# Column sums of an 8192x8192 matrix: summing rows on VectorE in fp32 instead of bf16 matmuls for every block, with the last two blocks in column strips

## Chip, cores, metric

The kernel runs on one core of one Trainium2 chip. The metric is device time in microseconds (us), the median of the executions. The profile's span runs from the first to the last instruction and is about 1.85 us shorter than the time (644.0 against 645.85 in the profiled run of before). The experiments ran on three chips, each beside the kernel before, so where two kernels differ by little, their ratios to before are the fairer measure.

Engines: PE is TensorE's matmuls, PEld its weight loads, DVE is VectorE, ACT is ScalarE, SPq is the queue on SyncE that issues the loads and stores. "Landing" is the moment when a load's data can be used. The "granted clock" is TensorE's clock as a share of full speed. PSUM is the memory in which the matmuls' sums stand here, SBUF that of all other tiles.

## The reference

```python
def setup_inputs():
    return {"x": np.random.randn(8192, 8192).astype(np.float32)}

def reference(x):
    return np.sum(x, axis=0)
```

The input has 268.4 MB. It has to be read once, and nothing else of size moves.

## The kernel before

Rows are taken in 64 blocks of 128, one row per partition, so that a block is 128x8192 fp32, 4 MiB. ScalarE and VectorE cast it to bf16, and TensorE sums over the partitions with a column of ones, adding all blocks up in PSUM.

```python
load_pool = ctx.enter_context(tc.tile_pool(name="loads", bufs=4))
bf_pool = ctx.enter_context(tc.tile_pool(name="bf", bufs=3))
# ... cut: other pools; ones is [128, 1] bf16, psum is [128, 4096] fp32 ...
nsplit = 4
CS = C // nsplit
for i in range(n_row_blocks):                      # 64 blocks
    xt = load_pool.tile([P, C], mybir.dt.float32)
    xb = bf_pool.tile([P, C], mybir.dt.bfloat16)
    nc.sync.dma_start(out=xt, in_=xr[i])
    for s in range(nsplit):                        # casts, ScalarE and VectorE in turn
        # ... cut: eng.copy / eng.tensor_copy of xb[:, s*CS:(s+1)*CS] ...
    for g in range(n_col_groups):                  # 16 groups of 512 columns
        # ... cut: groups 0-7 go to partition 0, groups 8-15 to partition 64 ...
        nc.tensor.matmul(out=psum[opart : opart + 1, off : off + N], lhsT=ones,
                         rhs=xb[:, g * N : (g + 1) * N],
                         start=(i == 0), stop=(i == n_row_blocks - 1))

res = out_pool.tile([P, HALF], mybir.dt.float32)
nc.vector.tensor_copy(out=res[0:1, :], in_=psum[0:1, :])
nc.scalar.copy(out=res[64:65, :], in_=psum[64:65, :])
nc.sync.dma_start(out=out[0:HALF], in_=res[0:1, :])
nc.sync.dma_start(out=out[HALF:C], in_=res[64:65, :])
```

## Time and profile before

| what | value | where it is read |
|---|---|---|
| time | 645.85 us (645.6 to 646.63) | the runs |
| first block lands | 13.09 us | timeline, first cast |
| from one landing to the next | 9.72 us, mean 9.74 | timeline, starts of the casts |
| last block lands | 626.86 us | chain of waits |
| from there to the end | 17.1 us | span minus landing |

These are lines of the page of before. In the first group the columns are busy time, its share of the span, and the count. The row of digits gives the busy share of the 16 DMA engines in 40 equal slices, in tenths.

```profile
span 644.0 us, 2724 instructions
PE 336.7 (52%) x1024; PEld 97.4 (15%) x1024; DVE 155.6 (24%) x129; ACT 241.6 (38%) x130; POOL 0.3 (0%) x5
...
DMA  9999999999999999999999999999999999999970
...
q1 hardware_dynamic: 9220, 268.47, 97.0%
...
DMA 88%; ACT 5%; issue 4%; PE 1%; DVE 1%; SPq 0%; ACTq 0%
```

The loads are the bound: the DMA row is full until the last two slices, PE, the busiest compute engine, is busy for only 52%, and the chain of what released what is DMA for 88%. At 9.72 us per 4 MiB block the loads run at 431 GB/s.

The end of the chain of waits of before (start, duration, what):

```profile
591.73 35.03 DMA xt<-in_x_dram
...
626.86 1.91 ACT xb L50
...
628.81 4.50 PE psum L60 x15
...
633.34 4.42 DVE res L69
...
637.78 3.56 ACT res L70
```

After the last landing at 626.86 everything is in series: casts, matmuls, two copies that each run along a single partition, and the last store, 2.6 us from its issue at 641.37 to the end.

### The profile page before, as it was taken

The page shows a single profiled execution, that of the slowest core. Times are in us where ns is not written, and L with a number is a line of the kernel's source. Part 1 is how long each engine was busy: PE and PEld are TensorE (multiplying, and loading weights), DVE is VectorE, ACT ScalarE, POOL GpSimd, SP SyncE. Part 2 cuts the span into 40 slices and gives each one's busy share as a digit, 9 for nine tenths or more (in the row PEclk, how much of TensorE's full clock was granted, in tenths as well). Part 3 has the DMA queues.
Part 4 walks back from the last instruction along what each step waited for, and adds up shares of the span by engine and source line. Part 5 has one row for each costly group of instructions (what it writes and reads, how often), then busy time and mean ns, then how long its engine had stood idle before and what let it go on. Part 6 is the DMA issues. An engine that isn't in the chain of part 4 may idle for free.

```text
span 644.0 us, 2724 instructions
## 1 busy us (share of the span) xinstructions
PE 336.7 (52%) x1024; PEld 97.4 (15%) x1024; DVE 155.6 (24%) x129; ACT 241.6 (38%) x130; POOL 0.3 (0%) x5
## 2 busy tenths in 40 slices
PE   1464653655545644654646546635555547446533
PEld 0111111111111111111111111101111111111110
DVE  1122122222221221221221221221221221222223
ACT  2243243342442442442442432433433433433423
POOL 0000000000000000000000000000000000000000
PEclk9767668667767687678676766676678676876686
DMA  9999999999999999999999999999999999999970
GB/s 387 427 423 440 435 427 423 444 432 426 426 440 434 422 429 442 429 425 433 438 429 427 434 431 432 429 436 434 426 429 430 438 427 430 429 438 429 434 339 2
DMA packets 9233, 268.64 MB, mean 417 GB/s; under 512 B 1026, under 2 KB 1026, under 8 KB 1026
## 3 DMA queue, kind: packets, MB, share of 16 engines
q1 hardware_dynamic: 9220, 268.47, 97.0%
q8 instruction: 8, 0.13, 0.1%
q14 instruction: 5, 0.04, 0.0%
HBM read 268.44 MB, written 0.03 MB: 417 GB/s over the span
## 4 chain that ended last, share of the span: by engine, by line
DMA 88%; ACT 5%; issue 4%; PE 1%; DVE 1%; SPq 0%; ACTq 0%
DMA xt<-in_x_dram 88%; ACT xb L50 5%; PE psum L60 1%; DVE res L69 1%; ACT res L70 1%; SPq L46 0%; ACTq L50 0%
## 5 line engine op out<-in xcount | busy, mean ns | idle before, releaser
L60 PE MATMUL psum<-xb,ones 128*1 128x512 bf16 x1024 | 336.7, 570 | 296.6 <-DVE xb L52 290.7
L50 ACT CAST xb<-xt 128x2048 bf16<-128x2048 f32 x128 | 236.7, 1896 | 391.8 <-DMA xt<-in_x_dram 391.8
L52 DVE CAST xb<-xt 128x2048 bf16<-128x2048 f32 x128 | 151.2, 1224 | 478.0 <-DMA xt<-in_x_dram 478.0
L60 PEld LDWEIGHTS <-ones 128*1 128x1 bf16 x1024 | 97.4, 107 | 535.3 <-issue 521.9
L70 ACT COPY res<-psum 1x4096 f32<-1x4096 f32 x1 | 3.6, 3564 | 7.2 <-DVE res L69 7.2
L69 DVE COPY res<-psum 1x4096 f32<-1x4096 f32 x1 | 4.4, 4411 | 4.1 <-PE psum L60 4.1
L50 ACT ACT_TABLE_LOAD x1 | 1.3, 1283 | 0.7 <-PEq L87 0.7
L37 POOL MEMSET ones<- 128x1 bf16 x1 | 0.1, 102 | 0.3 <-POOLq L87 0.3
L87 POOL MEMSET const-bfloat16-1.0<- 128x1 bf16 x1 | 0.1, 102 | 0.0
L87 POOL MEMSET const-uint8-127<- 128x1 uint8 x1 | 0.1, 102 | 0.0
L87 POOL MEMSET const-float32-0.0<- 128x1 f32 x1 | 0.1, 99 | 0.2 <-issue 0.2
L87 POOL MEMSET const-float32-1.0<- 128x1 f32 x1 | 0.1, 99 | 0.0
## 6 DMA issues: line engine op xcount, KB each, us to landing
xt<-in_x_dram SPq DMA_DIRECT2D x64, 4096.0 KB, 35.0
out_dram<-res SPq DMA_DIRECT2D x2, 16.0 KB
```

The lines of the kernel that those rows point to most:

```text
L37: nc.gpsimd.memset(ones, 1.0)
L50: eng.copy(out=xb[:, s * CS:(s + 1) * CS], in_=xt[:, s * CS:(s + 1) * CS])
L52: eng.tensor_copy(out=xb[:, s * CS:(s + 1) * CS], in_=xt[:, s * CS:(s + 1) * CS])
L60: nc.tensor.matmul(out=psum[opart : opart + 1, off : off + N], lhsT=ones, rhs=xb[:, g * N : (g + 1) * N], start=(i == 0), stop=(i == n_row ...
L69: nc.vector.tensor_copy(out=res[0:1, :], in_=psum[0:1, :])
L70: nc.scalar.copy(out=res[64:65, :], in_=psum[64:65, :])
L87: nc = _bacc.Bacc("TRN2", target_bir_lowering=False, num_devices=1)
```

## The change

Its intent: take the casts and matmuls out of the stream, keep the sum in fp32, and shorten the end. VectorE adds each block to an accumulator of 128x8192 fp32, in four adds of 2048 columns. Fp32 matmuls with ones sum over the partitions only at the end. The last two blocks are loaded together, as column strips of 4, 2, 1, 0.5 and 0.5 MiB, so that little work is left after the last landing. Each matmul has 32 equal output rows and goes to one of four groups of 32 partitions ("column groups" of TensorE, the index `j`), so that 512 columns end as 128 elements on each of four groups.

```diff
-    load_pool = ctx.enter_context(tc.tile_pool(name="loads", bufs=4))
-    bf_pool = ctx.enter_context(tc.tile_pool(name="bf", bufs=3))
+    load_pool = ctx.enter_context(tc.tile_pool(name="loads", bufs=3))
...
+STRIPS = [(0, 8), (8, 4), (12, 2), (14, 1), (15, 1)]      # first unit, units of 512 columns
+    xl = x[n_acc * P :, :].rearrange("(p k) c -> p k c", k=2)   # last two blocks, n_acc = 62
+    ones = const_pool.tile([P, 32], F32)
+    psum = psum_pool.tile([P, n_banks * 512], F32)         # one tile, four banks
+    acc = const_pool.tile([P, C], F32)
+    last = last_pool.tile([P, 2, C], F32)
...
+    first = None
+    for t in range(n_acc):
+        xt = load_pool.tile([P, C], F32, tag="xt")
+        nc.sync.dma_start(out=xt, in_=xr[t])
+        if t == 0:
+            first = xt
+            continue
+        other = first if t == 1 else acc
+        for b in range(n_banks):
+            nc.vector.tensor_tensor(out=acc[:, cols], in0=other[:, cols], in1=xt[:, cols], op=add)
+    for u0, nu in STRIPS:
+        nc.sync.dma_start(out=last[:, :, cols], in_=xl[:, :, cols])
+    for b in range(n_banks):          # accumulator: 16 fp32 matmuls of 512 columns
+        for j in range(NJ):
+            mm(v[:, j], j, 512 * b, 512, True, False)
+    for u0, nu in STRIPS:
+        # strips of 4 units or more: one add of the two rows on VectorE, then matmuls;
+        # narrower ones: matmuls for both rows
+        ...
+        nc.vector.tensor_copy(out=res[:, 128 * u0 : 128 * (u0 + nu)],
+                              in_=psum[:, 128 * u0 : 128 * (u0 + nu)])
+        nc.sync.dma_start(out=outr[:, u0 : u0 + nu, :], in_=res[0 : 97 : 32, ...])
```

(The diff is cut and its long lines are shortened; the casts, the bf16 matmuls and the two long copies of before are gone.)

More of the change, by code (lines that the diff above doesn't have):

```diff
@@ L7 @@
 from concourse._compat import with_exitstack
+F32 = mybir.dt.float32
+BANK = 2048
+NQ, NJ, NI = 4, 4, 128
+STRIPS = [(0, 8), (8, 4), (12, 2), (14, 1), (15, 1)]
 @with_exitstack
@@ L19 @@
     R, C = x.shape
-    assert R % P == 0
-    n_row_blocks = R // P
-    N = 512
-    assert C % N == 0
-    n_col_groups = C // N
-    HALF = C // 2
+    assert R % P == 0 and C % BANK == 0
+    n_blocks = R // P
+    n_banks = C // BANK
+    n_acc = n_blocks - 2
     xr = x.rearrange("(b p) c -> b p c", p=P)
+    xl = x[n_acc * P :, :].rearrange("(p k) c -> p k c", k=2)
+    outr = out.rearrange("(u j i) -> j u i", j=NJ, i=NI)
     const_pool = ctx.enter_context(tc.tile_pool(name="const", bufs=1))
-    load_pool = ctx.enter_context(tc.tile_pool(name="loads", bufs=4))
@@ L32 @@
-    bf_pool = ctx.enter_context(tc.tile_pool(name="bf", bufs=3))
-    psum_pool = ctx.enter_context(tc.tile_pool(name="psum", bufs=1, space=bass.MemoryType.PSUM))
-    out_pool = ctx.enter_context(tc.tile_pool(name="out", bufs=1))
-    ones = const_pool.tile([P, 1], mybir.dt.bfloat16)
-    nc.gpsimd.memset(ones, 1.0)
-    psum = psum_pool.tile([P, HALF], mybir.dt.float32)
-    nsplit = 4
-    CS = C // nsplit
-    for i in range(n_row_blocks):
-        xt = load_pool.tile([P, C], mybir.dt.float32)
-        xb = bf_pool.tile([P, C], mybir.dt.bfloat16)
-        nc.sync.dma_start(out=xt, in_=xr[i])
-        for s in range(nsplit):
-            eng = nc.scalar if s % 2 == 0 else nc.vector
-            if eng is nc.scalar:
-                eng.copy(out=xb[:, s * CS:(s + 1) * CS], in_=xt[:, s * CS:(s + 1) * CS])
-            else:
-                eng.tensor_copy(out=xb[:, s * CS:(s + 1) * CS], in_=xt[:, s * CS:(s + 1) * CS])
-        for g in range(n_col_groups):
-            if g < n_col_groups // 2:
-                opart = 0
-                off = g * N
-            else:
-                opart = 64
-                off = (g - n_col_groups // 2) * N
-            nc.tensor.matmul(
-                out=psum[opart : opart + 1, off : off + N],
-                lhsT=ones,
-                rhs=xb[:, g * N : (g + 1) * N],
-                start=(i == 0),
-                stop=(i == n_row_blocks - 1),
-            )
@@ L68 @@
-    res = out_pool.tile([P, HALF], mybir.dt.float32)
-    nc.vector.tensor_copy(out=res[0:1, :], in_=psum[0:1, :])
-    nc.scalar.copy(out=res[64:65, :], in_=psum[64:65, :])
-    nc.sync.dma_start(out=out[0:HALF], in_=res[0:1, :])
-    nc.sync.dma_start(out=out[HALF:C], in_=res[64:65, :])
+    load_pool = ctx.enter_context(tc.tile_pool(name="loads", bufs=3))
+    last_pool = ctx.enter_context(tc.tile_pool(name="last", bufs=1))
+    psum_pool = ctx.enter_context(
+        tc.tile_pool(name="psum", bufs=1, space=bass.MemoryType.PSUM)
+    )
@@ new lines, with mm @@
+    ones = const_pool.tile([P, 32], F32)
+    nc.gpsimd.memset(ones, 1.0)
+    psum = psum_pool.tile([P, n_banks * 512], F32)
+    res = const_pool.tile([P, n_banks * 512], F32)
+    acc = const_pool.tile([P, C], F32)
+    last = last_pool.tile([P, 2, C], F32)
+    add = mybir.AluOpType.add
+    def mm(rhs, j, lo, n, start, stop):
+        nc.tensor.matmul(
+            out=psum[32 * j : 32 * j + 32, lo : lo + n],
+            lhsT=ones,
+            rhs=rhs,
+            start=start,
+            stop=stop,
+            skip_group_check=True,
+        )
@@ new lines @@
+    first = None
[7 more added lines that the diff above has]
+        for b in range(n_banks):
+            cols = slice(b * BANK, (b + 1) * BANK)
+            nc.vector.tensor_tensor(
+                out=acc[:, cols], in0=other[:, cols], in1=xt[:, cols], op=add
+            )
+    for u0, nu in STRIPS:
+        cols = slice(u0 * 512, (u0 + nu) * 512)
+        nc.sync.dma_start(out=last[:, :, cols], in_=xl[:, :, cols])
@@ new lines @@
+    for b in range(n_banks):
+        v = acc[:, b * BANK : (b + 1) * BANK].rearrange("p (q j i) -> p j q i", q=NQ, j=NJ)
+        for j in range(NJ):
+            mm(v[:, j], j, 512 * b, 512, True, False)
+    for u0, nu in STRIPS:
+        cols = slice(u0 * 512, (u0 + nu) * 512)
+        for w in range(u0, u0 + nu, 4):
+            m = min(4, u0 + nu - w)
+            rows = [0, 1]
+            if nu >= 4:
+                wc = slice(w * 512, (w + m) * 512)
+                nc.vector.tensor_tensor(
+                    out=last[:, 0, wc], in0=last[:, 0, wc], in1=last[:, 1, wc], op=add
+                )
+                rows = [0]
+            for k in rows:
+                v = last[:, k, w * 512 : (w + m) * 512].rearrange(
+                    "p (q j i) -> p j q i", q=m, j=NJ
+                )
+                for j in range(NJ):
+                    mm(v[:, j], j, 128 * w, 128 * m, False, k == rows[-1])
+        nc.vector.tensor_copy(
+            out=res[:, 128 * u0 : 128 * (u0 + nu)], in_=psum[:, 128 * u0 : 128 * (u0 + nu)]
+        )
+        nc.sync.dma_start(
+            out=outr[:, u0 : u0 + nu, :],
+            in_=res[0 : 97 : 32, 128 * u0 : 128 * (u0 + nu)].rearrange(
+                "j (u i) -> j u i", i=NI
+            ),
+        )
```

## The prediction

> **What bounds the kernel now.** The page of before gives a span of 644.0 us; the DMA row reads 9 in 38 of 40 slices and the load queue takes 97.0% of the 16 engines' span, while PE is busy 52%, ACT 38%, DVE 24%. The chain of waits is 88% DMA. In the timeline ACT's casts start every 9.72 us (first block 13.09, last 626.86): 4 MiB per 9.72 us is 431 GB/s. One step takes 10.89. The Trainium skill ("DMA: Bandwidth & Descriptors", Specifications) puts the fabric ceiling at 435 GB/s; the trace agrees. So the loads cannot get faster; only the ends can change. After the last landing 17.1 us remain: casts 3.7, matmuls to 633.3, two one-partition evacuations in series (4.4 and 3.6), and 2.6 from the last store's issue to the end. Before the first landing, 13.1 us.
>
> **What the change does.** Removed: all 128+128 casts, 1,024 bf16 matmuls, the two long evacuations. The bytes stay. Added: 244 fp32 adds of 128x2048 on VectorE. The Trainium skill ("VectorE: DVE Perf Modes", the perf-mode tier table) gives 2293 ns for such an add; before has none, but its 2048-wide cast measures 1224 ns against the page's 1227, so I trust it. Four adds are about 9.2 us per 9.72 us block: DVE goes from 24% to about 88% busy and just keeps up. All of that stays off the critical path except in two places:
>
> 1. Start. Three buffers instead of four, and block 0's is held until block 1's adds end. Block 1 lands at 22.8, so block 3 is issued near 32.0. Issue to landing on an empty queue was 12.4 us (0.73 to 13.09), so it lands near 44.4 instead of 42.2: about +2 us, once. From then on each buffer is freed about 0.5 us before the next landing, with a whole block still in flight; the queue doesn't run dry.
>
> 2. Tail. The last 8 MiB arrive as strips of 4, 2, 1, 0.5, 0.5 MiB. After the last 0.5 MiB: eight 128-column fp32 matmuls (about 1.2 us, estimate from 0.43 us per 512 columns at the slow clock, four passes, four column groups side by side), a copy of 128x128 (0.3), a store (2.6): 4.3 us instead of 17.1. Gain about 13 us. Shorter DMA runs may cost 0.5 us.
>
> Sum on the span: 644.0 + 2.0 + 0.5 - 12.8 = 633.7; with the 1.85 us between span and measured time, 635.5 us. A 1.2 us hiccup of before may vanish with the 2,000 instructions of PE.
>
> **Predicted: 635.5 us, 8 in 10 between 632 and 645. Faster by over 2%: 0.20; within 2%: 0.77; slower by over 2%: 0.03.**
>
> **What shows it right or wrong.** The adds' mean near 2.29 us and DVE idle before them ended by the load; load landings 9.72 us apart, with one step near 12 us at block 3; in the queue's waits a visible gap only there; PE idle again before the last strip lands; last landing to end near 4.3 us.
>
> **What would make it wrong.** (a) The four column groups don't run side by side for fp32. Then the 36 equivalents of a 512-column matmul at four passes of 0.215 us need 31 us, PE starts only 17 us before the last landing, and works off a backlog for some 15 us after it: 650 us, no gain. If consecutive groups overlap by just one pass of four, about 642. This is the largest risk, and sets the upper end. (b) Adds above 2.43 us, beside DMA writes: DVE becomes the bound. (c) No start gap and a still shorter tail: 632. (d) 2 KB runs slow the last strips by several us.

## The result, and the profile after

The time fell from 646.06 us (645.6 to 646.63, 4 runs) to 637.21 us (636.68 to 637.43, 4 runs): ratio 0.9862, 95% interval 0.9848 to 0.9876, by the measure "within 2%". Here and below a ratio is the mean time of one kernel's fast runs over that of the kernel before's fast runs of the same rounds, so it isn't quite the ratio of the medians that stand beside it. Later, beside other kernels, the changed kernel took 637.28 us, ratio 0.9865.

The same lines of the page after, with VectorE's adds:

```profile
span 635.1 us, 709 instructions
PE 14.8 (2%) x104; PEld 2.9 (0%) x104; DVE 552.4 (87%) x252; POOL 0.3 (0%) x5
...
DMA  8999999999999999999999999999999999999993
...
q1 hardware_dynamic: 10372, 268.47, 98.2%
...
DMA 69%; DVE 29%; PE 1%; issue 0%; SPq 0%; DVEq 0%
...
L74 DVE TENSOR_TENSOR acc<-acc,xt 128x2048 f32<-128x2048 f32 x240 | 533.9, 2286 | 50.2 <-DMA xt<-in_x_dram 50.2
```

The DMA row is still full. VectorE went from 24% to 87%, and its adds waited only for loads (50.2 us in all). The 29% that VectorE has in the chain do not mean that it became the bound: with three buffers a load is issued when the adds of an earlier block end, so the chain passes through VectorE, while another load is in flight and keeps the DMA engines busy.

The start of the stream, from the timeline of after (start, duration of the four adds, and in brackets the idle time before them and what ended it):

```profile
22.89 8.90 DVE L74 TENSOR_TENSOR acc<-xt 128x2048 f32<-128x2048 f32 x4 [22.89 <-DMA xt<-in_x_dram]
32.55 8.90 DVE L74 TENSOR_TENSOR acc<-acc,xt 128x2048 f32<-128x2048 f32 x4 [0.76 <-DMA xt<-in_x_dram]
44.13 8.90 DVE L74 TENSOR_TENSOR acc<-acc,xt 128x2048 f32<-128x2048 f32 x4 [2.69 <-DMA xt<-in_x_dram]
```

From block 2 to block 3 it is 11.58 us instead of the 9.67 of the other steps, and VectorE idles 2.69 us. This is the predicted empty queue: block 0's buffer is held until block 1's adds end at 31.8.

The end of the chain of waits of after:

```profile
624.95 1.98 PE psum L55 x8
...
626.96 0.70 DVE res L102
...
627.70 1.98 PE psum L55 x16
...
629.70 0.43 DVE res L102
...
630.18 1.12 PE psum L55 x16
...
631.33 0.30 DVE res L102
...
631.68 0.69 PE psum L55 x16
...
632.39 0.29 DVE res L102
```

This is not the tail that was predicted. The last strip was issued at 589.87 and its load took 36.6 us from issue to landing, the maximum of the second line here (first a line of the timeline of SyncE: start, duration of the issue; then a line of the view of the tile `last`):

```profile
589.87 14.66 SPq L80 DMA_DIRECT2D last<-in_x_dram  x1
...
DMA to landing us min/median/max: 35.4/36.0/36.6
```

That puts the last landing at 626.5. From there it took 8.6 us to the end, and the chain is a zigzag: matmuls of strip 1, copy of strip 1, matmuls of strip 2, copy of strip 2, and so on. The waits between 620 and 636 us say the same (who waited, for whom: us in total, times, longest):

```profile
PEld psum L55 <- DVE res L102: 8.5, 4, 3.6
DVE res L102 <- PE psum L55: 6.1, 4, 2.1
PE psum L55 <- DVE res L102: 3.7, 4, 1.9
```

Four times, the matmuls of a strip waited for the *copy of the strip before*, although their own data had landed: the last three strips landed at 623.9, 625.2 and 626.5, and their matmuls began at 627.7, 630.2 and 631.7.

So the two traces differ by these terms on the span:

| term | predicted | measured | how |
|---|---|---|---|
| gap at block 3 | +2.0 | +1.9 | 11.58 - 9.67 |
| landing step | 0 | -2.5 | mean 9.742 before, 9.702 after without the gap, times 62 |
| strips load slower | +0.5 | +0.2 | last two blocks 606.93 to 626.5, less 2 x 9.67 |
| last landing | 629.4 | 626.5 | sum of the above on 626.86 |
| tail | 4.3 | 8.6 | 635.1 - 626.5 |
| span | 633.7 | 635.1 | |

The total was close by luck: two misses partly cancel. The loads ended 2.9 us earlier than predicted, and the tail was 4.3 us longer.

### The profile page after: what moved, and what is told of

Read it like the earlier page. It is cut to its first block, busy times and chain, and to the rows that moved or that the text cites. A ratio compares the mean times of both kernels' runs of the same rounds, so it can differ in the third digit from the quotient of the medians.

```text
span 635.1 us, 709 instructions
## 1 busy us (share of the span) xinstructions
PE 14.8 (2%) x104; PEld 2.9 (0%) x104; DVE 552.4 (87%) x252; POOL 0.3 (0%) x5
## 4 chain that ended last, share of the span: by engine, by line
DMA 69%; DVE 29%; PE 1%; issue 0%; SPq 0%; DVEq 0%
DMA xt<-in_x_dram 64%; DVE acc L74 28%; DMA last<-in_x_dram 5%; PE psum L55 1%; DVE res L102 0%; DVE last L92 0%; SPq L67 0%; SPq L80 0%; DVEq L74 0%
## 5 line engine op out<-in xcount | busy, mean ns | idle before, releaser
L74 DVE TENSOR_TENSOR acc<-acc,xt 128x2048 f32<-128x2048 f32 x240 | 533.9, 2286 | 50.2 <-DMA xt<-in_x_dram 50.2
L74 DVE TENSOR_TENSOR acc<-xt 128x2048 f32<-128x2048 f32 x4 | 8.9, 2287 | 22.9 <-DMA xt<-in_x_dram 22.9
L55 PE MATMUL psum<-acc,ones 128*32 128x512 f32 x32 | 6.2, 859 | 610.7 <-DVE acc L74 610.7
L55 PE MATMUL psum<-last,ones 128*32 128x128 f32 (+2 forms) x72 | 8.6, 599 | 6.8 <-DVE res L102 3.7
L102 DVE COPY res<-psum 128x128 f32<-128x128 f32 (+3 forms) x5 | 2.9, 583 | 6.1 <-PE psum L55 6.1
L92 DVE TENSOR_TENSOR last<-last 128x2048 f32<-128x2048 f32 x3 | 6.8, 2289 | 1.2 <-DMA last<-in_x_dram 1.2
L55 PEld LDWEIGHTS psum<-last,ones 128*32 128x32 f32 x72 | 2.1, 138 | 13.9 <-DVE res L102 8.5
```

Of the source, the lines that this page charges most:

```text
L55: nc.tensor.matmul(out=psum[32 * j : 32 * j + 32, lo : lo + n], lhsT=ones, rhs=rhs, start=start, stop=stop, skip_group_check=True,)
L74: nc.vector.tensor_tensor(out=acc[:, cols], in0=other[:, cols], in1=xt[:, cols], op=add)
L92: nc.vector.tensor_tensor(out=last[:, 0, wc], in0=last[:, 0, wc], in1=last[:, 1, wc], op=add)
L102: nc.vector.tensor_copy(out=res[:, 128 * u0 : 128 * (u0 + nu)], in_=psum[:, 128 * u0 : 128 * (u0 + nu)])
```

## The experiments

Theory: the gain is the rebuilt tail; it is cut by the start gap and by the zigzag over one PSUM tile. Rivals: the fp32 accumulation is what pays; the tail is set by late landings or a slow TensorE; three buffers are too few in any case. All kernels gave a correct result, except b2_no_mm. Each edit is against the changed kernel or, for names with b, c and e0, against the kernel before.

| run | time us | ratio to before, 95% interval |
|---|---|---|
| e1_block0_in_acc | 635.57 | 0.9845 (0.9831 to 0.9858) |
| e2_split_psum | 633.65 | 0.9810 (0.9797 to 0.9823) |
| e3_both | 630.02 | 0.9765 (0.9751 to 0.9779) |
| b1_bufs3 | 646.36 | 1.0010 (0.9996 to 1.0024) |
| b2_no_mm | 645.25 | 0.9994 (0.9981 to 1.0008) |
| b4_bf16_tail | 633.77 | 0.9817 (0.9804 to 0.9831) |
| a5_group_outer | 636.13 | 0.9855 (0.9841 to 0.9868) |
| a0_after_again | 637.28 | 0.9865 (0.9849 to 0.9882) |
| a6_three_strips | 637.27 | 0.9864 (0.9850 to 0.9879) |
| e4_warm | 630.11 | 0.9754 (0.9739 to 0.9768) |

e0_before_again and c1_dve_casts: 645.93 and 645.57 us.

### The start gap: e1_block0_in_acc

```diff
-        if t == 0:
-            first = xt
-            continue
-        other = first if t == 1 else acc
+    nc.sync.dma_start(out=acc, in_=xr[0])      # before the loop, which starts at block 1
```

> The changed kernel, with block 0 loaded straight into the accumulator, so that it holds no load buffer. Theory: the one step of 11.58 us at block 3 is the empty load queue, because block 0's buffer is held until block 1's adds end; it becomes 9.67 and the time falls by 1.9 us (to about 335.2 + 300, that is 635.3 us), and nothing else moves. Rival: the gap is only moved (three buffers are too few anyway, and the queue runs dry one block later): then the time stays at 637.2 +- 0.4 and another step is long.

("335.2 + 300" is a clumsy way to write 635.3.) Measured: 635.57 us, 1.7 us less than the changed kernel's 637.28. The timeline of this run, blocks 2 and 3:

```profile
32.34 8.90 DVE L71 TENSOR_TENSOR acc<-acc,xt 128x2048 f32<-128x2048 f32 x4 [0.77 <-DMA xt<-in_x_dram]
42.08 8.90 DVE L71 TENSOR_TENSOR acc<-acc,xt 128x2048 f32<-128x2048 f32 x4 [0.84 <-DMA xt<-in_x_dram]
```

The step of 11.58 is now 9.74, no other step took over its length (the long ones, 10.06, 9.96 and 10.65, stand in the changed kernel too, as 10.09, 9.85 and 10.65), and VectorE idles 0.84 us instead of 2.69. The intervals of the two ratios overlap; the times don't (635.51 to 635.86 against 637.01 to 637.34), and the trace shows where the difference lies. The gap was the held buffer, and three buffers are enough afterwards, though VectorE is busy 8.9 of every 9.7 us.

### The zigzag: e2_split_psum and e3_both

```diff
-    psum = psum_pool.tile([P, n_banks * 512], F32)
-    res = const_pool.tile([P, n_banks * 512], F32)
+    ps, rs = {}, {}
+    for u0, nu in STRIPS:
+        ps[u0] = psum_pool.tile([P, max(512, 128 * nu)], F32, name=f"ps{u0}")
+        rs[u0] = const_pool.tile([P, 128 * nu], F32, name=f"rs{u0}")
```

The accumulator's matmuls are cut at the strips' borders to fit; e3_both has the edit of e1 as well.

> The changed kernel, with one PSUM tile (its own banks) and one result tile for each strip instead of one PSUM tile for all. Theory T1: the tail of 8 to 9 us after the last landing, where 4.3 had been predicted, is a zigzag: each strip's matmuls wait for the copy of the strip before, because all strips write one PSUM tile. Then the strips' matmuls wait for their own loads, the last copy ends about 2 us after the last landing, and the time falls by 4 to 5 us, to 632.5 +- 0.7. Rival T2: the tail is the late landing of the last strips (short DMA runs) and PE's slow clock: then at most 1 us falls away, and the time stays above 636.

> Both edits. They touch different ends of the kernel, so the gains should add: 637.2 - 1.9 - 4.5 = 630.8 +- 0.8 us, over 2% faster than before. If the edits shared a cause, it would be above 631.8.

Measured: 633.65 us for e2, which is 3.6 less than the changed kernel (expected 4 to 5, to 632.5 +- 0.7: the theory holds, the size is a little short), and 630.02 us for e3, within the expected range and 2.35% faster than before. The plain sum of the gains would be 637.28 - 1.7 - 3.6 = 632.0, and e3 lies 2 us below it; the next section says what that probably is. The end of the chain of waits in e2:

```profile
621.50 2.30 DVE last L99
...
623.85 4.64 PE ps L58 x56
...
628.51 0.29 DVE rs L109
```

And in e3's profiled run:

```profile
619.73 2.30 DVE last L96
...
622.07 4.87 PE ps L58 x56
...
626.97 0.29 DVE rs L106
```

(The line before these in each chain is the load.) The copies are gone from the chain; one unbroken run of 56 matmul records takes their place, and one copy of 0.29 us ends it. Strip 1's matmuls now start when its add ends. The Trainium skill ("PSUM — Partial Sum Buffer", section "PSUM bank collisions raise a hardware error") asks that two engines never use the same bank and quadrant at once. Strips 2, 3 and 4 shared a bank, so they needed either a wait or, as here, banks of their own. Strips 0 and 1 lay in different banks and strip 1's matmuls waited all the same (until 624.9, the end of copy 0): that wait came from the one tile, not from the banks. No run separates the two for the other strips.

### TensorE's clock in the tail: e4_warm

```diff
+    junk = psum_pool.tile([P, 512], F32, name="junk")   # nobody reads it
+            # after each full slice of acc and each half of strip 0:
+            for j in range(NJ):
+                warm(v[:, j], j)      # the same matmul again, into junk
```

> Both edits (one PSUM tile per strip, block 0 into the accumulator), and after each slice of the accumulator and each half of the first strip its matmuls once more into a PSUM bank that nobody reads: work without use, in TensorE's idle time. Theory (in the version with both edits, TensorE at half clock is the last link: its matmuls run without a pause from 622.1 to 626.9 while the last data have landed by about 624.7, because its clock drops in the gaps before): the granted clock stays at 1.0 to the end, the last matmul ends 1 to 1.7 us sooner, and the time is 628.3 to 629.2 us against 630.0. Rival (the matmuls wait for the loads, the clock matters nothing): 630.0 +- 0.3.

Measured: 630.11 us, against 630.02 for e3: no gain in the median, so the expectation of 628.3 to 629.2 failed. The traces of the profiled runs, and the executions one by one, say why. A window of e3's tail (columns: window, length, busy time of PE, PEld, DVE and POOL, granted clock, DMA share, GB/s):

```profile
624.00:626.00 2.00, 2.00 (x29) 1.05 (x24) 0.91 (x2) 0.00 (x0) 0.50 0.04 13
```

The same window of e4:

```profile
624.00:626.00 2.00, 1.01 (x32) 0.48 (x20) 1.01 (x3) 0.00 (x0) 1.00 0.06 18
```

And the end of e4's chain of waits:

```profile
588.05 36.61 DMA last<-in_x_dram
...
624.71 0.69 PE ps L70 x16
...
625.42 0.29 DVE rs L124
```

In e3's profiled run TensorE has half the clock in the tail and is the last link; in e4 it has the full clock and the last link is the landing itself (the load, 0.69 us of matmuls, a copy, the store). But e3's profiled run was its slowest: 631.92 us with a mean clock of 0.994 over the whole span; its other three runs took 629.94 to 630.09 at 0.996 to 0.997. All four of e4 took 629.97 to 630.18 at 1.000. So the extra matmuls give nothing where e3 was quick already. That they also remove its slow executions is likely, but one slow run in four against none in four doesn't show it. (e3 and e4 ran on different chips; their ratios to before, 0.9765 and 0.9754, have overlapping intervals too.) In e4 the tail, from the last landing at 624.7 to the end of the span at 628.3, is 3.6 us: without the shared tile and at full clock it is even shorter than the 4.3 us predicted.

The Trainium skill ("TensorE: Matmul & The Clock Gate", Part 1) says that the clock gate opens and closes in a free-running window of activity, so that the same kernel can meet it differently from run to run; a mean clock that differs between executions of one kernel agrees with it. The clock is the likely reason for the 2 us by which e3 lies below the sum of its parts. e2 ran at 0.994 or 0.995 in all its runs, and at half clock in its traced tail. e3's profiled run, in the same condition, has a span of 629.9 us against e2's 631.7, about the start gap alone; e3's quick runs have 628.0 to 628.2. As an estimate, a mean clock of 0.997 instead of 0.994 over 630 us means 3.8 us less at half clock, and so some 1.9 us gained if all of it falls into the tail. It isn't shown: no trace of a quick e3 execution was taken, and one run of e2 took 632.57 us at the same mean clock as two of the others, so the mean clock, rounded as it is, doesn't tell all.

### The tail without the accumulation: b4_bf16_tail

The kernel before, with casts and bf16 matmuls for all 64 blocks, and only its end rebuilt:

```diff
-        nc.sync.dma_start(out=xt, in_=xr[i])
+        last = i == n_row_blocks - 1
+        for s in range(nsplit if last else 1):
+            cols = slice(s * CS, (s + 1) * CS) if last else slice(0, C)
+            nc.sync.dma_start(out=xt[:, cols], in_=xr[i][:, cols])
...
+                out=ps[b][32 * j : 32 * j + 32, :],     # one PSUM tile for each strip of 2048 columns
...
+    for b in range(NB):
+        nc.vector.tensor_copy(out=res[b], in_=ps[b])    # 128x512 each, stored by itself
```

(In the last block both engines cast half of each strip.)

> One part of the change alone: the kernel before keeps its casts and bf16 matmuls, and only its tail is rebuilt. The last block is loaded in four strips of 2048 columns, each cast by both engines; the sums lie in four PSUM tiles of one bank, on four column groups, so that each is evacuated as 128x512 and stored by itself. Theory (the gain of the change is its tail, the accumulation on VectorE brings next to nothing): the time after the last landing goes from 17.1 us to about 5, and the time to 634 +- 1, at or below the changed kernel's 637.2. Rival (the accumulation in fp32 is what pays): the time stays above 641.

Measured: 633.77 us, as expected, and below the changed kernel's 637.28. The end of its chain of waits:

```profile
593.02 33.92 DMA xt<-in_x_dram
...
626.96 1.05 ACT xb L56
...
628.06 0.64 PE ps L66 x4
...
628.72 0.69 DVE res L76
```

The last landing is that of before (626.96 against 626.86), and the end comes 5.0 us after it (span 632.0), where before needed 17.1. So the time that the change gains can be had from the tail alone, with VectorE left as it was. What the accumulation brings of its own is fp32 sums, and the faster landing step, to which we come.

### Are the column groups needed? a5_group_outer

```diff
-    for b in range(n_banks):
-        for j in range(NJ):
+    for j in range(NJ):
+        for b in range(n_banks):
             mm(v[:, j], j, 512 * b, 512, True, False)
```

(and the strips' matmuls sorted by `j` too.)

> The changed kernel, with the same matmuls in another order: all of one column group before those of the next, so that neighbours share a group. Tests the largest risk named in the prediction. Theory (four fp32 matmuls on four column groups run side by side, 1.06 to 1.94 us for the four; on one group they run one after the other): the 16 matmuls of the accumulator take 14 us or more instead of about 6, TensorE is behind when the last strip lands, and the time rises by 8 to 15 us, to 645 to 652. Rival (fp32 matmuls of 32 columns are fast by themselves, the groups don't matter): the time stays at 637.2 +- 1.

Measured: 636.13 us. Both expectations missed: it did not get slower, and if anything faster by 1 us (its interval overlaps that of the changed kernel). The rival's range missed it by less than 0.1 us only, but its reason, that the groups don't matter, is refuted by the traces below. The timeline of its weight loads:

```profile
616.29 0.11 PEld L55 LDWEIGHTS psum<-acc,ones 128*32 128x32 f32 x1 [0.32 <-issue]
616.72 0.11 PEld L55 LDWEIGHTS psum<-acc,ones 128*32 128x32 f32 x1 [0.32 <-issue]
617.15 0.11 PEld L55 LDWEIGHTS psum<-acc,ones 128*32 128x32 f32 x1 [0.32 <-issue]
617.58 0.14 PEld L55 LDWEIGHTS psum<-acc,ones 128*32 128x32 f32 x3 [0.32 <-issue]
```

And the accumulator's last four matmuls in the changed kernel, where the groups alternate, at the same full clock:

```profile
615.88 1.06 PE L55 MATMUL psum<-acc,ones 128*32 128x512 f32 x8 [0.92 <-DVE acc L74]
```

A fp32 matmul of 512 columns shows as two records, so eight records are four matmuls. Within one group a record comes every 0.43 us, so a matmul takes 0.86 us alone; four of them on four groups take 1.06 us together, where one after another they would take 3.4. The first half of the theory is shown: the groups do run side by side. The Trainium skill agrees on both counts: "FP8 and Floating Point Precision", section "TensorE Precision Notes", gives true fp32 four passes (0.86 us is four times 0.216 us, the distance from one bf16 matmul of 512 columns to the next at full clock, in the trace of before from 18.00 us on), and "TensorE: Matmul & The Clock Gate", Part 3, describes matmuls on different column groups as concurrent. The second half, a backlog, fell: the 13 matmuls of the accumulator that were left at 615.83 were through at 622.95, in 7.1 us and not 13 x 0.86 = 11.2, because at the borders between groups matmuls overlap again (three weight loads within 0.43 us from 617.58). TensorE, which now worked without gaps, also kept its full clock longer (a mean of 0.998 to 1.000 in all runs, against 0.986 to 0.992), and strip 1's matmuls took 1.06 us instead of 1.94 later on. Why the overlap at the borders is so large was not settled.

### Is the narrowing worth anything here? a6_three_strips, with a0_after_again

```diff
-STRIPS = [(0, 8), (8, 4), (12, 2), (14, 1), (15, 1)]
+STRIPS = [(0, 8), (8, 4), (12, 4)]
```

> The changed kernel, unchanged, on the chip of the last runs, for comparison with them: 637.2 +- 0.6 us, with one step of 11.5 us at block 3, one of 10.65 and two near 10.05.

> The changed kernel with its last three strips (1, 0.5 and 0.5 MiB) joined into one of 2 MiB: one strip is added on VectorE, and the chain of copies and matmuls has three links instead of five. Theory (in the changed kernel the narrow strips pay little, because each brings a link to the zigzag between TensorE and VectorE over one PSUM tile): after the last landing near 626.2 an add of 2.3, matmuls of 1.9, a copy of 0.7 and a store of 2.5 end at 633.6, that is 635.6 us or 1.5 us less than the changed kernel. Rival (narrow strips shorten the tail, as intended): the time rises by 2 us or more, above 639.

Measured: 637.28 us for the changed kernel again and 637.27 us with three strips. Neither expectation: the last three strips neither pay nor cost. The last add stood in VectorE's order behind the copy of strip 1 and started at 627.69, which is 1.2 us after the last landing (626.5, as in the changed kernel); this takes up most of the gain that I had expected. The narrow strips, meant to shorten the tail, give back in links of the zigzag what they save. With PSUM tiles of their own, no run tells what they are worth.

### The landing step: e0_before_again, b1_bufs3, b2_no_mm, c1_dve_casts

The changed kernel's blocks land every 9.67 us and before's every 9.72: small, but over 62 blocks 2.5 us with the single long steps counted in, and not predicted.

> The kernel before, unchanged, profiled on the chip that runs the others. Question: is the 9.72 us from landing to landing of before (against 9.67 in the changed kernel) its own or that of another chip? Theory R1 (the kernel's own doing: something that before does beside the loads costs 0.5%): 9.72 again, while the others of this call show 9.67. Rival R2 (chip or moment): the same step as the others of this call, within 0.01.

Measured: 9.72 in the middle (the few long steps apart, 9.70 to 9.74) on the chip that ran e1, e2 and e3, whose steps lie at 9.67 in the middle. It is before's own doing (R1).

```diff
-    load_pool = ctx.enter_context(tc.tile_pool(name="loads", bufs=4))
+    load_pool = ctx.enter_context(tc.tile_pool(name="loads", bufs=3))
```

> The kernel before with three load buffers instead of four, as in the changed kernel. Question: what makes the landing step 9.72 us in before and 9.67 in the changed kernel? Theory Q (the depth of the load queue: before keeps three blocks queued, the changed kernel two): the step becomes 9.67 and the time falls by about 2.5 us, to 643.2. Rival S (the casts, the matmuls or their instructions beside the loads): the step stays at 9.71 to 9.72 and the time at 645.5 to 646.5.

Measured: 9.71 to 9.72, and 646.36 us. It isn't the depth of the queue.

```diff
-        for g in range(n_col_groups):
+        for g in range(n_col_groups if i in (0, n_row_blocks - 1) else 0):
```

> The kernel before with matmuls for the first and the last block alone; the result is wrong on purpose. The casts stay. If the matmuls (TensorE's reads, or the fetching of its 2,000 instructions) cost the 0.5% of the load rate, the step becomes 9.67 and the time about 643. If the casts cost it, the step stays at 9.72 and the time within 0.7 us of 645.7. If the one step of 10.9 us is due to TensorE's instructions, it goes here.

Measured: 9.71 to 9.72, and 645.25 us, so the matmuls don't cost the step. The step of 10.9 us and the three of 10.0 in before's trace (all by the starts of ScalarE's casts) did vanish, and others came, one of 10.47 and, at the very end, one of 9.99. The first belongs to the matmuls in some way: it stands near 72.6 us in the traces of before, e0, b1, b4 and c1 (10.83 to 11.11) and is missing in b2's. Fetching TensorE's instructions may be how (in before, one 20 KB packet of an instruction queue falls between 60 and 80 us), but one coincidence doesn't show it.

```diff
-            eng = nc.scalar if s % 2 == 0 else nc.vector
+            eng = nc.vector
```

> The kernel before with all casts on VectorE (four of 1.2 us for each block), ScalarE idle until the end. The landing step of before is 9.72 us, that of the changed kernel 9.67; the depth of the queue and the matmuls are ruled out. Theory A (ScalarE's traffic): the step becomes 9.67 and the time about 643. Rival B (the casts themselves, whichever engine does them, or another thing): the step stays at 9.71 to 9.72.

Measured: 9.71 to 9.72. It isn't ScalarE's traffic. Left are the casts as such (with bf16 written to SBUF beside the loads, though the adds of the changed kernel write twice as many bytes) and things that I didn't think of; the cause stays open. It is worth at most 2.5 us.

## Why the prediction was right, and where it was not

The range and the class were right, and the change of -8.9 us is close to the forecast of -10.35. That closeness is partly luck: the tail was mis-sized by 4.3 us, and loads that came 2.9 us sooner than forecast hid most of it. By the points of the prediction:

- *The loads bound the kernel, and only the ends can change.* Right in the main: the DMA row is full before and after, and b4_bf16_tail gets the gain from the end alone. But "the loads cannot get faster" was wrong: the mean step went from 9.742 to 9.702 us, 0.4%, which gave 2.5 us, and why is open.
- *DVE at about 88%, adds near 2.29 us, just keeping up.* Right: 87%, 2.286 us. The tier table of the Trainium skill's "VectorE: DVE Perf Modes" (2293 ns) agrees with this trace. Back to back, four adds took 8.90 and not 9.2 us.
- *Start gap of about +2 us, once.* Right: 1.91 us, and e1_block0_in_acc takes it away.
- *Shorter runs may cost 0.5 us.* About 0.2.
- *Tail of 4.3 us instead of 17.1.* This is the term that was mis-sized: 8.6 us were measured. The sum "matmuls, a copy, a store" after the last landing was right as the work of the last strip (from 631.68 to the end, 3.4 us), but I took it that this work starts when the strip lands. In fact it starts when the four copies and matmuls ahead of it are through, since all strips wrote one PSUM tile, and with TensorE at half clock until 631.2 us on top (strip 1: 1.94 us for what takes 1.06 at the full clock). e2_split_psum takes the wait away and gains 3.6 us. I had looked at the order of instructions before predicting and seen VectorE's semaphore among the waits of the small strips' matmuls, which needed nothing from VectorE; that was the sign, and I passed over it.
- *PE idle again before the last strip lands.* Wrong, for the same reason.
- *Largest risk: column groups don't run side by side for fp32.* They do (a5_group_outer: four in 1.06 us, one in 0.86).
- *The 1.2 us hiccup may vanish.* It is gone from its place, but one step of 10.65 and one or two of 10.0 to 10.2 are in the traces of the changed kernel and its variants. Whether they are the same thing, and their cause, is open.

The best version, e3_both, is 2.35% faster than before. Of its gain the accumulation can claim, by this account, at most the landing step; the rest is the tail.

## What to carry to other kernels

When loads fill the whole span, cost a change from the last landing on, and write down what the last piece waits for besides its data: a shared PSUM tile turned five independent strips into one chain and gave back 3.6 of the 12.8 us that the new tail was to gain. A buffer that is held "just for the first block" empties the load queue once; load the first block into the accumulator itself. And when a large rewrite gains 1.4%, try its smallest part alone: here a new tail on the old kernel gained more than the rewrite.

## What the Trainium skill lacked or had wrong

- "DMA: Bandwidth & Descriptors", section "Bandwidth": one sentence says that for transfers between HBM and SBUF the HBM side (about 358 GB/s) binds. That doesn't hold for one core alone, and the section itself limits it elsewhere: it gives 425 GB/s for 16 MB on a single core, and about 358 for each of two cores that stream together. Here one core streams 4 MiB loads at 431 to 434 GB/s, close to the fabric figure of 435 of the same page.
- The same page has nothing on how many loads a queue takes before the issue of the next is held up: of the five strip loads the first four took about 0.6 us each to issue and the fifth 14.66 us, behind some 15 MiB of loads that had not landed. It did no harm here, because nothing behind it was urgent; that the queue was full is my reading.
- "TensorE: Matmul & The Clock Gate" has no time for a fp32 matmul: 0.86 us for 512 columns at the full clock, as two records, and 1.06 us for four on four column groups.
- "PSUM — Partial Sum Buffer" tells when a wait by bank is needed, not that a program can hold a wait over a shared tile without need: strip 1's matmuls, in a bank of their own, waited until 624.9 us for the copy of strip 0.
- No page explains why a stream of equal loads takes 9.72 us per block beside bf16 casts and 9.67 beside fp32 adds.
